# Query, score and choice pieces beside the expert gathers: one planned sequence becomes two streams with fixed places, and head 1's queries move ahead of the gathers

## The chip, the core and the metric

The kernel runs on one core of one Trainium2 chip. The metric is the device time of one execution in microseconds (us), as the median of the runs shown. One execution was taken by the hardware profiler; its times are the trace that everything below is read from.

## What is computed

Two transformer-like blocks on 256 tokens of width 1024, each with its own mixing branches. The change touches the last part of the second block alone, a retrieval of single-neuron experts. Cut to what matters:

```python
PEER_HEADS = 8; PEER_KEYS = 128; PEER_TOPK = 16
def _peer(h, w_q, sub_keys, u_emb, v_emb):
    q = (tok @ w_q).reshape(n_tok, PEER_HEADS, 2, PEER_HALF)
    s = jnp.einsum('nhpc,hpkc->nhpk', q, sub_keys)
    s_top, i_top = lax.top_k(s, PEER_TOPK)
    cand = s_top[:, :, 0, :, None] + s_top[:, :, 1, None, :]        # 16 x 16 per head
    best, pos = lax.top_k(cand, PEER_TOPK)
    expert = jnp.take_along_axis(cand_idx, pos, axis=-1)            # 16 experts per token and head
    gate = jax.nn.softmax(best, axis=-1)
    act = jax.nn.gelu(jnp.einsum('tkd,td->tk', u_emb[expert], tok)) * gate
    return jnp.einsum('tk,tkd->td', act, v_emb[expert])
x = x + _peer(_rmsnorm(x, norm2_g), ...)
return _rmsnorm(x, final_g)
```

Each token fetches 8 x 16 = 128 experts, and each expert is a row of 1024 numbers (u) and one of 1024 (v).

## The kernel before

Tokens lie in two blocks of 128 (b = 0, 1), one token per partition. The heads are worked in five groups (n): head 0, head 1, heads 2-3, 4-5, 6-7. An **item** is one gather of one expert per token of a block: 128 rows of 2048 numbers, 1 MiB, so 256 items in all. They come in the order group, block, head, expert: items 0-15 and 16-31 are head 0 (blocks 0 and 1), 32-63 head 1, 64-127 group 2, 128-191 group 3, 192-255 group 4.

`fetch` (L1470-1478) lets GpSimd (POOL) write and start the gather of an item into one of 8 slots of a ring (tag "uv", RING = 8). `use` (L1480-1492) is an item's work: VectorE (DVE) multiplies the u half with the token and sums (L1485, written into the slot itself), ScalarE (ACT) takes the gelu, the gate and a diagonal matrix `dg` (L1486, L1487, L1489), and TensorE (PE) adds dg x v to the block's sums `acc` with four matmul records (L1491). After that the slot is free for the gather eight items later.

Which expert rows a group needs is found by three kinds of pieces, which stand between the items:

- **queries** (`queries`, L1419-1441): four weight tiles of 128x1024 are split into a rounded part and a rest (L245 on ACT, then L246 on DVE; three buffers each), each is followed by 24 matmuls of 128x256 (L267-269), and the result `pq` is copied out by ACT (L1426). For head 1 the weights (wqa) are loaded here by SP's queue and there are two tiles; those of the other groups (wq) lie in SBUF.
- **scores** (`scores`, L1406-1416): the queries against the keys `sk` (L1412) into `psco`, copied by ACT into `s` (L1414).
- **choices** (`topk`, L1313-1369), once per group and block: per key half a best-16 piece (L1320-1324), per head a candidate piece (L1336 and again L1320-1324 on 256 wide rows), two one-hot pieces (L1341-1356, the second ends with `rows`, which the gathers read), and a softmax piece (L1364-1368: DVE `mx`, ACT exp with a table load, DVE reciprocal and `gate`).

`plan` (L1456-1461) chains all of them in one sequence: for each group its queries, scores, choices of block 0, choices of block 1. The main loop (L1506-1510) uses an item, takes one step of that sequence after items 0-7 and after every second later item (two of three between items 40 and 63), and fetches item i + 8; when its rows aren't there yet, `fetch` takes steps until they are. PE, DVE and ACT execute this part in the order in which it is written (`manual_schedule`). Every engine works through its own list in order, so an instruction that waits holds back all that is behind it on its engine.

Ahead of the loop, `first_queries` (L1284-1305) makes the queries and scores of head 0, and transposes the tokens into `acc` (L1304); then come the choices of (0, 0). `factors` and `tokens` (L1383-1397) make the normalized tokens `hn` with the norm weights `n2`, which lie in a weight buffer (tag "wf", four of them). This part, and all before, is put in order by the scheduler.

## Time and profile before

| | us |
|---|---|
| median of 3 runs (1533.45 to 1537.11) | 1534.99 |
| the profiled execution, whole | 1536.1 |
| its span in the trace | 1534.3 |
| first gather starts (POOL) | 852.1 |
| last product on DVE starts | 1522.9 |

The span is what the trace covers from its first to its last instruction, and 1.8 us of the whole lie around it. Busy shares over the whole span are PE 89%, DVE 68%, ACT 48%, POOL 20%, but they mix two very different parts: up to about 843 us PE multiplies almost without a pause, and from 852 us on the gathers run. Of the forty slices of the page, 38.4 us each, the transfer rate of the 24th to the 39th lies between 369 and 422 GB/s. A row of a timeline is: start, duration, engine, line, operation, output and inputs, number of instructions merged, and in brackets the idle time just before with what ended it. A row of a table by stretch holds for each engine the busy time and the number of instructions, then TensorE's granted clock, the share of the transfer engines, and GB/s.

### The profile page before, as it was taken

How to read it: one execution, taken by the hardware profiler on the slowest of the kernel's cores; microseconds unless marked ns; L12 is line 12 of the kernel's file. 1: busy time of each engine (PE TensorE's matmuls, PEld its weight loads, DVE VectorE, ACT ScalarE, POOL GpSimd, SP SyncE). 2: the span in 40 equal slices, each digit the busy share in tenths (PEclk: the TensorE clock that was granted, in tenths of full speed). 3: DMA queues.
4: the chain of work that ended last, by engine and by line, in shares of the span. 5: the costliest groups of instructions: out<-in, count | busy, mean ns of one | idle time of the engine just before them, and what ended most of it. 6: DMA issues, size and time to landing. Idle time of an engine off the chain costs nothing.

```text
span 1534.3 us, 21082 instructions
## 1 busy us (share of the span) xinstructions
PE 1359.4 (89%) x7496; PEld 975.3 (64%) x7496; DVE 1043.9 (68%) x2095; ACT 735.9 (48%) x1560; POOL 311.4 (20%) x277
## 2 busy tenths in 40 slices
PE   6999999989999999999999487877887888877786
PEld 3787799989999988989889142523533533322222
DVE  6775676867766778646387777588588588544543
ACT  7622454456555675534464435444443444433433
POOL 0000000000000000000010346344454455533341
PEclk9999999999999999999999799999999999999999
DMA  8655376745555453312155799999999999999996
GB/s 296 220 184 173 121 246 204 241 141 183 182 188 181 139 176 100 122 53 86 43 187 205 306 413 421 372 391 413 369 397 421 420 378 421 421 421 421 421 422 269
DMA packets 76712, 413.07 MB, mean 269 GB/s; under 512 B 8656, under 2 KB 9040, under 8 KB 43456
## 3 DMA queue, kind: packets, MB, share of 16 engines
q0 software_dynamic: 38880, 276.59, 44.2%
q1 hardware_dynamic: 37584, 134.88, 26.3%
q8 instruction: 59, 0.97, 0.2%
q14 instruction: 45, 0.37, 0.1%
q10 hardware_dynamic: 144, 0.26, 0.0%
HBM read 410.66 MB, written 1.05 MB: 268 GB/s over the span
## 4 chain that ended last, share of the span: by engine, by line
PE 55%; DVE 15%; DMA 11%; issue 9%; ACT 5%; POOL 5%; POOLq 0%; SPq 0%; DVEq 0%; ACTq 0%
PE psb L267 9%; PE psb L268 9%; PE psb L269 9%; DMA uv<-in_uv_dram,rows 9%; DVE uv L1485 6%; POOL uv L1478 5%; PE acc L1491 4%; PE psa L277 2%; PE psa L279 2%; PE psa L278 2%; DMA wf<-in_wmod_dram 2%; PE acc L267 1%; PE acc L268 1%; PE acc L269 1%; PE psr L1032 1%
## 5 line engine op out<-in xcount | busy, mean ns | idle before, releaser
L1491 PE MATMUL acc<-uv,dg 128*128 128x512 f32 x1024 | 495.3, 622 | 141.2 <-ACT dg L1489 140.7
L1491 PEld LDWEIGHTS acc<-uv,dg 128*128 128x128 f32 x1024 | 185.5, 194 | 438.2 <-ACT dg L1489 276.8
L1485 DVE CUSTOM_DVE_ANT_0 uv<-uv,hn 128x1024 f32<-128x1024 f32 x256 | 307.0, 1220 | 118.7 <-DMA uv<-in_uv_dram,rows 116.2
L1478 POOL DMA_INDIRECT uv<-in_uv_dram,rows x256 | 299.5, 1170 | 395.3 <-PE acc L1491 269.2
L246 DVE TENSOR_TENSOR wl<-wf,wh 128x1024 fp32r<-128x1024 f32 x213 | 258.2, 1216 | 134.4 <-ACT wh L245 131.6
L245 ACT CAST wh<-wf 128x1024 fp32r<-128x1024 f32 x213 | 221.9, 1044 | 240.4 <-PE psb L268 146.5
L267 PE MATMUL psb<-hxh,wh 128*128 128x256 f32 x960 | 280.8, 293 | 3.6 <-ACT hxh L370 3.4
L268 PE MATMUL psb<-hxl,wh 128*128 128x256 f32 x960 | 274.0, 286 | 0.0
L269 PE MATMUL psb<-hxh,wl 128*128 128x256 f32 x960 | 273.6, 286 | 0.2 <-DVE wl L246 0.2
L1486 ACT ACTIVATE act<-act 128x1 f32<-128x1 f32 x256 | 51.8, 202 | 325.1 <-DVE act L1485 325.1
L267 PEld LDWEIGHTS psb<-hxh,wh 128*128 128x128 f32 x960 | 184.9, 193 | 10.5 <-issue 5.2
L268 PEld LDWEIGHTS psb<-hxl,wh 128*128 128x128 f32 x960 | 184.9, 193 | 4.2 <-issue 3.3
L269 PEld LDWEIGHTS psb<-hxh,wl 128*128 128x128 f32 x960 | 184.6, 193 | 1.0 <-issue 0.3
L1489 ACT ACTIVATE dg<-io,act 128x128 f32<-128x128 f32 x256 | 102.8, 402 | 8.4
L1487 ACT ACTIVATE act<-act,gate 128x1 f32<-128x1 f32 x256 | 75.4, 294 | 8.3
L970 POOL MEMSET mt<- 128x2048 f32 x2 | 3.5, 1804 | 352.4 <-PE psb L268 352.4
L833 POOL DMA_DIRECT2D wq<-in_wq_dram x12 | 6.3, 529 | 262.4 <-PE pstm L982 142.8
L478 DVE SCALAR_TENSOR_TENSOR macc<-wf,cs,macc 128x512 f32<-128x512 f32 x56 | 41.9, 748 | 17.7 <-DMA wf<-in_wmod_dram 17.0
L267 PE MATMUL acc<-fh,wh 128*128 128x256 f32 x176 | 49.5, 281 | 0.0
L268 PE MATMUL acc<-fl,wh 128*128 128x256 f32 x176 | 49.5, 281 | 0.0
L269 PE MATMUL acc<-fh,wl 128*128 128x256 f32 x176 | 49.4, 281 | 0.0
L279 PE MATMUL psa<-wh,hxl 128*128 128x512 f32 x96 | 38.4, 400 | 0.0
(461 smaller groups left out, 2072.2 us busy)
## 6 DMA issues: line engine op xcount, KB each, us to landing
wf<-in_wmod_dram SPq DMA_DIRECT2D x48, 512.0 KB, 4.3
wf<-in_wup_dram SPq DMA_DIRECT2D x44, 512.0 KB, 3.6
wf<-in_win_dram SPq DMA_DIRECT2D x28, 512.0 KB, 4.5
wf<-in_wdn_dram SPq DMA_DIRECT2D x22, 512.0 KB, 3.7
wf<-in_wbg_dram SPq DMA_DIRECT2D x16, 512.0 KB, 4.4
wf<-in_wo_dram SPq DMA_DIRECT2D x16, 512.0 KB, 4.6
wf<-in_wml_dram SPq DMA_DIRECT2D x16, 512.0 KB, 3.5
wf<-in_wg_dram SPq DMA_DIRECT2D x16, 512.0 KB, 3.5
```

The source lines that it names most:

```text
L245: self.nc.scalar.copy(h, src)
L246: self.nc.vector.tensor_sub(l, src, h.bitcast(F32))
L267: nc.tensor.matmul(ps, p, xh[:, k0 + k, :], start=s, stop=False, skip_group_check=True)
L268: nc.tensor.matmul(ps, p, xl[:, k0 + k, :], start=False, stop=False, skip_group_check=True)
L269: nc.tensor.matmul(ps, q, xh[:, k0 + k, :], start=False, stop=e, skip_group_check=True)
L279: nc.tensor.matmul(ps, y, wh[:, k, :n], start=False, stop=e)
L1478: nc.gpsimd.indirect_dma_start(t, None, a["uv"], bass.IndirectOffsetOnAxis(ap=self.rows[b][:, h, k:k + 1], axis=0))
L1485: nc.vector.tensor_tensor_reduce(t[:, :D], t[:, :D], hn[:, b], 1.0, 0.0, ALU.mult, ALU.add, act)
L1486: nc.scalar.activation(act, act, AF.Gelu)
L1487: nc.scalar.activation(act, act, AF.Copy, scale=self.gate[b][:, h, k:k + 1])
L1489: nc.scalar.activation(dg, ident, AF.Copy, scale=act)
L1491: nc.tensor.matmul(acc[b][c], dg, t[:, D + c * 512:D + (c + 1) * 512], start=False, stop=h == PH - 1 and k == TOPK - 1, skip_group_check=True)
```

## The change

- Head 1's two weight tiles are loaded and split with head 0's, and `first_queries` makes head 1's queries and scores too, after the transposes into `acc`. Queries, keys and scores of both heads take three weight buffers; `n2` moves from a weight buffer into the ring's first slot. So 7 gathers start ahead of `tokens` and the 8th after it.
- The one sequence becomes two streams. Stream 0 holds the choices, each with a first item and a distance of 2 (1 for the first); stream 1 the queries and scores of groups 2, 3 and 4, from items 14, 70 and 134, one step every 4 items. The copy of `pq` stands one step (4 items) behind the last 24 matmuls, and the scores one step behind that copy.
- The softmax piece is cut in two: the reciprocal and `gate` stand one step behind `mx` and the exp.
- Behind the last item a Sqrt of one number per partition is added on ACT.

```diff
-        for _ in range(2):
-            self.ahead.append(self.weights(a["wqa"][0][:, 4 * len(self.ahead):4 * len(self.ahead) + 4], 256, 4))
+        for i in range(4):
+            self.ahead.append(self.weights(a["wqa"][i // 2][:, 4 * (i % 2):4 * (i % 2) + 4], 256, 4))
...
+        qs, sk, ss = (self.wp.tile([P, 1024], F32, tag="wf", name=n, bufs=4).rearrange("p (a t) -> p a t", t=P) for n in "qks")
+        nc.sync.dma_start(sk[:, :4], self.a["skt"][:, :4])
+        self.s0 = []
+        for h in range(2):
...
+            self.lin(self.a["wqa"][h], KT, 256, bs=[(self.scaled, cq)])
+            for b in range(NB):
...
+            if h:
+                break
+            for b in range(NB):
+                for k in range(KT):
+                    nc.tensor.matmul(self.acc[b][k // 4][:, k % 4 * P:(k % 4 + 1) * P], xt[:, k, b * P:(b + 1) * P], self.ident,
+                                     start=k % 4 == 0, stop=False, skip_group_check=True)
...
             nc.scalar.activation(bv[:, h], bv[:, h], AF.Exp, bias=mx[:, h:h + 1], scale=r, accum_out=sm[:, h:h + 1])
+        yield
         nc.vector.reciprocal(sm, sm)
...
-        n2 = self.wp.tile([P, 1024], F32, tag="wf", name="n2", bufs=4)
+        n2 = bp.tile([P, 2 * D], F32, tag="uv", name="n2", bufs=RING)[:, :D]
...
-            for k in range(2 if n == 1 else 4):
...
+            u = self.lin_units(None, KT, 512, bs=[(self.scaled, cq)])
+            for k in range(4):
+                self.ahead.append(self.weights(None, raw=next(wq)))
+                if k:
                     next(u)
                 yield
+            next(u)
+            yield
             for _ in u:
                 pass
             yield
             choices[n] = scores(q, sk, h0, nh)
             yield
...
-        def plan():
-            for n in range(len(heads)):
-                if n:
-                    yield from queries(n)
-                for b in range(NB):
-                    yield from run(n, b)
...
+        streams = [[], []]
+        for n, b, i, d in ((0, 1, 0, 1), (1, 0, 7, 2), (1, 1, 20, 2), (2, 0, 40, 2), (2, 1, 62, 2), (3, 0, 100, 2), (3, 1, 128, 2),
+                           (4, 0, 164, 2), (4, 1, 192, 2)):
+            streams[0].append([i, d, choose(n, b) if n < 2 else lambda n=n, b=b: choose(n, b)])
+        for n, i in ((2, 14), (3, 70), (4, 134)):
+            streams[1].append([i, 4, queries(n)])
...
-            for _ in range(RING):
+            for _ in range(RING - 1):
                 fetch()
+            next(start)
             tokens(0)
-            next(planned)
             tokens(1)
+            fetch()
+            for _ in start:
+                pass
             for i, w in enumerate(work):
                 use(w)
-                if i < 8 or (i % 3 if 40 <= i < 64 else i % 2):
-                    next(planned, None)
+                advance(0, i)
+                advance(1, i)
                 fetch()
+
+            nc.scalar.activation(self.warm, self.r[:, :1], AF.Sqrt)
```

Where the pieces stand is seen in each engine's list. **ACT, queries of group 2.** `pq` are the queries, `psb` the sums of the matmuls, `act` and `dg` an item's work, `s` the scores. Before:

```order
L1489 ACTIVATE dg_9585<-io_76,act_9581 128x128
L1486 ACTIVATE act_9591<-act_9591 128x1
L1487 ACTIVATE act_9591<-act_9591,gate0_8780 128x1
L1489 ACTIVATE dg_9595<-io_76,act_9591 128x128
L1426 COPY pq_9447<-psb_9477 128x512
L1426 COPY pq_9448<-psb_9478 128x512
L1486 ACTIVATE act_9627<-act_9627 128x1
L1487 ACTIVATE act_9627<-act_9627,gate0_8780 128x1
L1489 ACTIVATE dg_9631<-io_76,act_9627 128x128
L1414 COPY s_9640<-psco_9635 128x512
L1414 COPY s_9647<-psco_9642 128x512
```

After, the same copies of `pq`:

```order
L1483 ACTIVATE dg_9525<-io_76,act_9521 128x128
L1433 COPY pq_9158<-psb_9217 128x512
L1433 COPY pq_9159<-psb_9218 128x512
L1480 ACTIVATE act_9533<-act_9533 128x1
L1481 ACTIVATE act_9533<-act_9533,gate0_8851 128x1
L1483 ACTIVATE dg_9537<-io_76,act_9533 128x128
L1480 ACTIVATE act_9543<-act_9543 128x1
L1481 ACTIVATE act_9543<-act_9543,gate0_8851 128x1
L1483 ACTIVATE dg_9547<-io_76,act_9543 128x128
```

Before, one item stands between the two pairs of copies; after, four do (two are shown), and the copies of `pq` stand four items behind the last matmuls that they read.

**PE, ahead of the first item.** `acc<-io,xt` are the transposes, `psco` the scores, `psb` the queries. Before:

```order
L269 MATMUL psb<-hxh,wl 128x256
L1304 MATMUL acc<-io,xt 128x128 x4
L1300 MATMUL psco<-q 128x128 x4
L1304 MATMUL acc<-io,xt 128x128 x12
L1491 MATMUL acc<-uv,dg 128x512 x16
L267 MATMUL psb<-hxh,wh 128x256
```

After, first where the transposes end and then, 48 matmuls of L267-269 later, where the items begin:

```order
L1308 MATMUL acc<-io,xt 128x128 x4
L1301 MATMUL psco<-k,q 128x128 x4
L1308 MATMUL acc<-io,xt 128x128 x12
L267 MATMUL psb<-hxh,wh 128x256
L268 MATMUL psb<-hxl,wh 128x256
```

```order
L267 MATMUL psb<-hxh,wh 128x256
L268 MATMUL psb<-hxl,wh 128x256
L269 MATMUL psb<-hxh,wl 128x256
L1301 MATMUL psco<-k,q 128x128 x4
L1485 MATMUL acc<-uv,dg 128x512 x38
```

Head 1's 48 matmuls and its scores now stand behind the transposes and ahead of the first item.

**DVE, ahead of the choices of (0, 0).** `wl` is the rest of a weight tile, `hxl` the rest of the scaled tokens, `xt` the tokens. Before:

```order
L246 TENSOR_TENSOR wl<-wf,wh 128x1024 x3
L842 TENSOR_TENSOR xt<-psb,xt 128x512 x2
L379 SCALAR_TENSOR_TENSOR hxl<-xt,cv_5305,hxh 128x256 x4
L1320 MAX sv<-s 128x8 x2
L1321 MAX_INDEX si<-sv,s 128x8 x2
```

After:

```order
L246 TENSOR_TENSOR wl<-wf,wh 128x1024 x3
L842 TENSOR_TENSOR xt<-psb,xt 128x512 x2
L246 TENSOR_TENSOR wl<-wf,wh 128x1024
L379 SCALAR_TENSOR_TENSOR hxl<-xt,cv_5305,hxh 128x256 x4
L246 TENSOR_TENSOR wl<-wf,wh 128x1024
L1324 MAX sv<-s 128x8 x2
```

One of head 1's two rests stands ahead of `hxl`, the other behind it.

## Rows read from the trace of the kernel before

**Rows 1.** Table by stretch from the first full rate to the last gathers.

```profile
865.00:985.00 120.00, 100.17 (x303) 48.40 (x304) 84.22 (x198) 53.80 (x151) 54.63 (x42) 0.96 1.01 418
985.00:1000.00 15.00, 11.92 (x56) 7.67 (x55) 6.95 (x25) 6.79 (x21) 4.32 (x4) 1.00 0.71 260
1000.00:1090.00 90.00, 69.57 (x188) 30.70 (x187) 73.68 (x189) 42.10 (x122) 44.18 (x36) 1.00 1.01 412
1090.00:1125.00 35.00, 31.72 (x120) 17.89 (x119) 23.29 (x63) 14.32 (x46) 16.34 (x14) 1.00 0.89 335
1125.00:1225.00 100.00, 80.60 (x247) 38.53 (x245) 77.51 (x184) 44.17 (x129) 49.43 (x39) 1.00 1.01 422
1225.00:1250.00 25.00, 21.89 (x62) 10.60 (x63) 17.70 (x55) 12.12 (x40) 12.21 (x11) 1.00 0.93 351
1250.00:1510.00 260.00, 206.54 (x416) 74.11 (x414) 153.07 (x309) 104.39 (x332) 109.49 (x104) 0.97 1.01 421
```

**Rows 2.** Transfers issued from 820 us on: number, KB each, us to landing.

```profile
wf<-in_wqa_dram SPq DMA_DIRECT2D x4, 512.0 KB, 4.8
sk<-in_skt_dram SPq DMA_DIRECT2D x3, 256.0 KB, 7.5
```

**Rows 3.** Timeline around the first dip, DVE, ACT and POOL.

```profile
982.10 1.22 DVE L1485 CUSTOM_DVE_ANT_0 uv<-uv,hn 128x1024 f32<-128x1024 f32 x1
986.27 0.59 ACT L1426 COPY pq<-psb 128x512 f32<-128x512 f32 x1 [5.38 <-issue]
991.47 0.94 POOL L1478 DMA_INDIRECT uv<-in_uv_dram,rows  x1 [5.45 <-PE acc L1491]
992.13 0.58 ACT L1414 COPY s<-psco 128x512 f32<-128x512 f32 x1 [2.96 <-PE psco L1412]
992.74 0.29 DVE L1320 MAX8 sv<-s 128x8 f32<-128x128 f32 x1 [9.41 <-ACT s L1414]
```

**Rows 4.** Timeline of DVE: products with a split between them, then with a candidate piece.

```profile
1080.22 1.22 DVE L1485 CUSTOM_DVE_ANT_0 uv<-uv,hn 128x1024 f32<-128x1024 f32 x1
1083.41 1.22 DVE L246 TENSOR_TENSOR wl<-wq,wh 128x1024 fp32r<-128x1024 f32 x1 [1.97 <-ACT wh L245]
1084.56 1.22 DVE L1485 CUSTOM_DVE_ANT_0 uv<-uv,hn 128x1024 f32<-128x1024 f32 x1
...
1122.96 1.22 DVE L1485 CUSTOM_DVE_ANT_0 uv<-uv,hn 128x1024 f32<-128x1024 f32 x1
...
1126.95 1.21 DVE L1485 CUSTOM_DVE_ANT_0 uv<-uv,hn 128x1024 f32<-128x1024 f32 x1
```

**Rows 5.** Start of the gathers: two table rows (granted clock third from last), then timelines.

```profile
830.00:840.00 10.00, 10.00 (x86) 10.00 (x85) 5.32 (x8) 3.72 (x6) 0.00 (x0) 1.00 0.21 67
...
852.00:855.00 3.00, 0.00 (x0) 0.00 (x0) 2.38 (x6) 1.77 (x3) 2.26 (x3) 0.50 0.41 104
...
832.70 1.05 ACT L245 CAST wh<-wf 128x1024 fp32r<-128x1024 f32 x1 [1.74 <-PE psb L268]
...
836.27 1.66 DVE L379 SCALAR_TENSOR_TENSOR hxl<-xt,cv,hxh 128x256 fp32r<-128x256 f32 x4
...
843.03 2.84 PE L1304 MATMUL acc<-io,xt 128*128 128x128 f32 x24
...
852.13 1.00 POOL L1478 DMA_INDIRECT uv<-in_uv_dram,rows  x1 [38.48 <-issue]
...
855.00 0.33 SPq L257 DMA_DIRECT2D wf<-in_wqa_dram  x1
...
857.70 1.23 DVE L1485 CUSTOM_DVE_ANT_0 uv<-uv,hn 128x1024 f32<-128x1024 f32 x1 [2.73 <-DMA uv<-in_uv_dram,rows]
```

**Rows 6.** Timeline of ACT behind the last item.

```profile
1526.29 0.60 ACT L1519 ACTIVATE o<-acc 128x512 f32<-128x512 f32 x1 [1.22 <-PE acc L1491]
...
1527.92 1.28 ACT L1523 ACT_TABLE_LOAD   x1
...
1529.21 0.29 ACT L1523 ACTIVATE r<-r,eps 128x1 f32<-128x1 f32 x1
```

More of the change, by code (lines that the diff above doesn't have):

```diff
@@ L1287, in first_queries, with cq @@
         self.acc = [[self.ps("acc") for _ in range(2)] for _ in range(NB)]
[L1288 to L1305 removed]
+        qs, sk, ss = (self.wp.tile([P, 1024], F32, tag="wf", name=n, bufs=4).rearrange("p (a t) -> p a t", t=P) for n in "qks")
+        nc.sync.dma_start(sk[:, :4], self.a["skt"][:, :4])
+        self.s0 = []
+        for h in range(2):
+            q = qs[:, 4 * h:4 * h + 4].rearrange("p (i b) t -> p i (b t)", i=2)
+            def cq(ps, n0):
+                nc.scalar.copy(q, ps)
+            self.lin(self.a["wqa"][h], KT, 256, bs=[(self.scaled, cq)])
+            for b in range(NB):
+                s = ss[:, 4 * h + 2 * b:4 * h + 2 * b + 2]
+                ps = self.psd("psco").rearrange("p (a t) -> p a t", a=4)
+                for i in range(2):
+                    nc.tensor.matmul(ps[:, i], q[:, i, b * P:(b + 1) * P], sk[:, 2 * h + i], start=True, stop=True)
+                nc.scalar.copy(s, ps[:, :2])
+                self.s0.append(s)
+            if h:
[4 more added lines that the diff above has]
+                                     start=k % 4 == 0, stop=False, skip_group_check=True)
     def k2(self, shape, name, dt=F32):
@@ L1426, in cq @@
                 nc.scalar.copy(q[n0 // 2], ps)
-            for k in range(2 if n == 1 else 4):
-                if n == 1:
-                    w = self.weights(a["wqa"][1][:, 4 * k:4 * k + 4], 256, 4)
-                else:
-                    w = self.weights(None, raw=next(wq))
-                self.ahead.append(w)
-                if k == 0:
-                    u = self.lin_units(None, KT, 256 * nh, bs=[(self.scaled, cq)])
-                else:
+            u = self.lin_units(None, KT, 512, bs=[(self.scaled, cq)])
+            for k in range(4):
+                self.ahead.append(self.weights(None, raw=next(wq)))
+                if k:
                     next(u)
                 yield
+            next(u)
+            yield
             for _ in u:
@@ L1443, in queries, with choose @@
             yield
-        choices = {}
-        todo = []
+        choices = {n: [self.topk(self.s0[2 * n + b], b, n, 1) for b in range(NB)] for n in range(2)}
         done = set()
-        def run(n, b):
+        def choose(n, b):
             for p in choices[n][b]:
@@ L1454, in run @@
                 yield
-        def plan():
-            for n in range(len(heads)):
-                if n:
-                    yield from queries(n)
-                for b in range(NB):
-                    yield from run(n, b)
-        planned = plan()
         work = [(n, b, h, k) for n, (h0, nh) in enumerate(heads) for b in range(NB) for h in range(h0, h0 + nh) for k in range(TOPK)]
@@ L1475, in fetch @@
             while (n, b) not in done:
-                next(planned)
+                advance(0)
             tiles[w] = t = bp.tile([P, 2 * D], F32, tag="uv", name="uv", bufs=RING)
@@ L1492, in use, with advance @@
                                  stop=h == PH - 1 and k == TOPK - 1, skip_group_check=True)
+        streams = [[], []]
[4 more added lines that the diff above has]
+            streams[1].append([i, 4, queries(n)])
+        def advance(j, i=None):
+            st = streams[j]
+            if st and (i is None or i >= st[0][0]):
+                x = st[0]
+                if callable(x[2]):
+                    x[2] = x[2]()
+                x[0] += x[1]
+                if next(x[2], 0) == 0:
+                    st.pop(0)
+                    advance(j, i)
         self.first = None
-        choices[0] = [self.topk(self.s0[b], b, 0, 1) for b in range(NB)]
+        start = choose(0, 0)
         factors()
```

19 lines of the change are left out of this document (1 added, 18 removed).

## The prediction

> **What bounds the kernel now.** I first read the transfer rate of the forty slices on the page, then a table by stretch of the part that the change touches, then the timelines of its dips, its start and its end. Between 1250 and 1510 us the transfers run at 421 GB/s with all 16 engines full, while PE, DVE and ACT have time to spare [rows 1]. An item is 128 x 2048 x 4 bytes = 1.049 MB, so the plateau gives one item per 1.049 / 0.421 = 2.49 us, and 256 of them need 637 us. Nothing that the engines do makes this stage shorter than that; what the change can win is where the rate falls below the plateau, plus bytes that aren't gathers, plus what stands ahead of and behind the stage.
>
> The rate falls at three places [rows 1]. Counted as (421 - rate) / 421 x length: 985 to 1000 us loses 161/421 x 15 = 5.7 us, 1090 to 1125 us 86/421 x 35 = 7.1, 1225 to 1250 us 70/421 x 25 = 4.2: 17.0 in all. The stretches beside them lose little: 865 to 985 us 0.9, 1000 to 1090 us 1.9, and 1125 to 1225 us nothing. Together 19.8 us.
>
> The timeline shows what the first dip is [rows 3]. ACT reaches the copy of `pq` and stands 5.38 us, since PE still has to do the last 24 query matmuls, which are behind items. Behind that copy on ACT are the items' gelu and `dg`, and PE's `acc` matmuls wait for those. One item later the score copy waits another 2.96 us for PE. DVE has run ahead through landed tiles, the last at 982.10, and stands 9.41 us in front of the first best-16 piece, which wants those scores. So slots come free late: POOL waits 5.45 us for PE before it starts the gather of 991.47, where one every 2.49 us is wanted. The eight slots run dry and the rate falls. The other two dips fall on the queries and scores of groups 3 and 4, which are written the same way.
>
> **The change part by part.** The sum is made against the profiled execution: 1536.1 us, of which 1534.3 are the span. Its differences are then put on the median of 1534.99, 1.1 below it.
>
> *The three dips.* In the new order the last 24 matmuls of a group, the copy of `pq` and the scores are each 4 items apart, that is 4 x 2.49 = 10 us at the plateau; the copy's wait was 5.38 us and the scores' 2.96 [rows 3], so both are over before ACT arrives. The first best-16 piece stands two items behind the scores for group 2 (items 38 and 40) and six for groups 3 and 4 (94 and 100, 158 and 164). Two items are 5 us, against 2.96 for PE's scores plus 0.58 for a copy. The waits that emptied the ring go: 19.8 us.
>
> *What is late next.* Query steps now run beside choices, so DVE gets both. From the product starts [rows 4]: an item alone takes 1.14 us (the rest of two neighbours' spacing), an item with a split 1084.56 - 1080.22 = 4.34, so a split adds 3.20, of which 1.97 is the wait for ACT's rounding; an item with a candidate piece takes 1126.95 - 1122.96 = 3.99, so that piece adds 2.85. Where a split stands behind a piece, ACT rounds during the piece, and the split adds 1.22. I price each one-hot piece at the candidate's 2.85 as a bound. The worst place is items 70 to 79: a pair of items has 2 x 2.49 = 4.98 us; items 70-71 need 2.28 + 2.85 + 1.22 = 6.35, 72-73 need 5.13, 74-75 6.35, 76-77 5.13, 78-79 2.28 + 3.20 = 5.48. DVE falls behind by 1.37 + 0.15 + 1.37 + 0.15 + 0.50 = 3.5 us and then catches up, since a pair without a piece needs 2.28. Items 134 to 143 are alike. What the ring forgives is read from the first dip: DVE stood 9.41 us and the transfers lost 5.7 there, or 7.6 with the stretch behind it, so 1.8 to 3.7 us are forgiven [rows 1, 3]. A loss between nothing and 2 x (3.5 - 1.8) = 3.4 us is left; the stretch of 1125 to 1225 us, which held splits at every second item at 422 GB/s, is nearest, so I take 1.0. PE is not near its limit: 24 query matmuls at 86 in 10 us [rows 5] are 2.8 us, now once in 10 us.
>
> *Could rows come too late?* A choice takes eight steps at every second item, so group 2's rows for block 0 are written behind item 54 and first fetched behind item 56; the others have 6 to 12 items to spare. DVE writes them ahead of the products whose slot that gather needs, so the slot still comes last. Nothing.
>
> *Bytes.* One of head 1's two weight loads (0.52 MB) starts at 855.00, when gathers already run [rows 5]; it now comes earlier, and so does one key load of 0.26 MB [rows 2]. 0.79 MB at 421 GB/s are 1.9 us less; between 0 (were they moved in a gap that is there anyway) and 1.9 I take 1.9, since the first gathers are in flight at 855.
>
> *Ahead of the first gather.* Added are two loads, two splits, 48 matmuls, a copy of `q`, four score matmuls and two copies. The 48 matmuls, 48 x 0.116 = 5.6 us [rows 5], stand behind the transposes, which end at 843.03 + 2.84 = 845.87 [rows 5]; PE is free from there until the first product, which DVE begins at 857.70. They and the scores end near 853, and ACT's exp, now behind their copies, near 855: hidden while the first gather is on its way, which costs 5.6 us from its start at 852.13. If that cover were gone they would cost some 8 us. The first new split is not hidden: ACT's cast of 1.05 us needs the buffer that the last `w_out` matmuls free, about 2.8 us after the one before it was let go at 832.70, so it begins near 835.5 and delays the scaled tokens by 0.9; on DVE its rest of 1.22 us stands ahead of `hxl` and moves it from 836.27 to about 837.8. PE needs those only for its second 24 query matmuls, from about 838.2; I estimate 0.3 us, between 0 and the 1.5 by which `hxl` moves. On SP's queue the keys for group 2 wait for the second split, and `n2` is queued behind them: it starts near 841 and is wanted by `tokens` at 852. The ring's first slot is held by `n2`, so the eighth gather waits for `tokens`, about 855; POOL comes to it at about 861. Nothing.
>
> *The end.* The Sqrt's table load of 1.28 us stands on the path at 1527.92 [rows 6]. It now runs in the 1.22 us that ACT waits until 1526.29; load and Sqrt take 1.28 + 0.29 = 1.57 and so push the squares back by about 0.4, so 0.9 are won, between 0 and 1.28. Between that load's start and the next instruction's at 1529.21 lie 1.29 us [rows 6]. The Trainium skill (ScalarE: Activation LUTs, What ACT_TABLE_LOAD costs) gives 1283 ns for such a load and another 1380 ns for a drain, some 2.7 us for each switch; the trace agrees on the load and shows no drain behind it. With the page's drain the gain would be an estimated 1.4 us more and the sum -22.7 (1512.3); I keep to the row.
>
> *The softmax piece.* DVE no longer waits for the exp. At the plateau such waits are covered by the ring: nothing.
>
> **Sum.** -19.8 + 1.0 - 1.9 + 0.3 - 0.9 = -21.3 us. The profiled execution would take 1514.8, the median 1513.7. With each term at its good end it is 19.8 + 1.9 + 1.3 = 23.0 less, 1512.0; with each at its bad end 19.8 - 3.4 - 1.5 = 14.9 less, 1520.1.
>
> **The rivals.** *The overlap empties the ring.* If queries beside choices drain the slots twice (items 70-82 and 134-146), each as deep as the mildest dip of before, 4.2 us, the gain on the dips is 19.8 - 8.4 = 11.4 and the time 1534.99 - 11.4 - 1.9 - 0.9 + 0.3 = 1521.1. For it: DVE needs up to 6.35 us per 4.98 there, and a late PE adds to it. Against: the dips came from a wait of 9.41 us, and no wait of that kind is left.
>
> *The dips stay.* POOL starts each gather itself, in 0.94 us alone [rows 3]. The Trainium skill (SBUF — State Buffer, the "DVE blocks DMA" trap) says that some DVE operations lock GpSimd out of a shared port while it writes descriptors; by that rule work of DVE beside the gathers, of which the change leaves as much as there was, makes the dips. In the trace DVE stood idle in the first dip and POOL waited for PE's `acc`, not for DVE [rows 3], which speaks against POOL and DVE as the cause. As a mechanism of this kernel: if the dips are POOL's and stay, only bytes, end and start count, 1534.99 - 1.9 - 0.9 + 0.3 = 1532.5.
>
> *Slower: the front comes onto the path.* Should the products wait for all of head 1's front work, that is two splits of 1.05 + 1.22 (4.5 us), 48 matmuls (5.6, or 11.2 at the granted clock of 0.50 that PE has at 852 us, after its pause) and, on SP's queue, a key load of 7.5 and the norm weights behind it at about 4.8 (a weight load's landing), the first product comes 22.4 to 28.0 us later. From 21.6 us on it eats up the gain (21.3 and the 0.3 already counted); at the near end the time is 1535.8, at the far end 1534.99 - 21.6 + 28.0 = 1541.4. Against it: PE has 11.8 us free between 845.87 and 857.70, and SP's two loads run while DVE still chooses.
>
> **How the numbers follow.** Forecast 0.81, overlap 0.12, dips stay 0.04, slower 0.03. A measurement of this kernel can tell about 0.2%, 3.1 us, from no change. Faster by more: 0.81 + 0.12 and half of the third case, 0.95; the other half within, 0.02; slower 0.03. The range goes from 1511.0 (1 us below the good end, for what 855 to 865 us may give) to 1522.0, which takes in the overlap; some 0.1 to 0.15 is left outside.
>
> **What would show it.** Right: no stretch of 15 us between 870 and 1490 us below 400 GB/s; copies of `pq` and best-16 pieces that wait under 1 us; first gather at 852 to 854; no table load behind the last item's `acc`. Wrong: dips at items 70-82 or 134-146 with DVE busy (overlap), dips with POOL busy (descriptors), or a first product later than 859 (front).

## The result, and the profile after

The changed kernel takes 1519.64 us in the median (1517.43 to 1521.7, 4 runs), the kernel before beside it 1536.05 (1533.45 to 1538.03, 4 runs): a ratio of 0.9894, 95% interval 0.9872 to 0.9916, or 16.4 us less. The forecast was 21.3 us less and 1513.7; the time lies in the range, 6 us above the forecast. The profiled execution is the run of 1517.43, its span 1515.7.

First the table by stretch, with the stretches of [rows 1] and two more at the end. Columns: the stretch, its length, busy time and instructions of PE, PE's weight loads, DVE, ACT and POOL, then granted clock, share of the 16 transfer engines, GB/s.

```profile
865.00:985.00 120.00, 101.12 (x300) 47.87 (x300) 91.33 (x235) 57.21 (x164) 58.07 (x47) 0.99 1.01 421
985.00:1000.00 15.00, 9.90 (x23) 3.99 (x23) 14.09 (x35) 5.42 (x18) 6.61 (x6) 1.00 1.01 419
1000.00:1090.00 90.00, 75.62 (x234) 36.91 (x233) 65.02 (x148) 44.01 (x127) 37.97 (x35) 0.98 1.01 416
1090.00:1125.00 35.00, 30.56 (x79) 12.94 (x77) 20.62 (x49) 13.80 (x45) 17.01 (x16) 1.00 1.01 418
1125.00:1225.00 100.00, 77.69 (x183) 30.58 (x184) 77.67 (x190) 40.76 (x125) 41.07 (x39) 1.00 1.01 421
1225.00:1250.00 25.00, 23.66 (x107) 14.93 (x107) 15.32 (x27) 14.23 (x40) 11.61 (x9) 1.00 1.01 401
1250.00:1490.00 240.00, 186.33 (x402) 68.81 (x400) 149.52 (x329) 98.86 (x310) 101.43 (x97) 1.00 1.01 422
1490.00:1500.00 10.00, 7.94 (x16) 2.71 (x16) 4.93 (x8) 3.63 (x13) 0.78 (x1) 1.00 0.77 321
1500.00:1515.00 15.00, 7.93 (x16) 2.71 (x16) 5.47 (x10) 6.48 (x17) 0.00 (x0) 0.98 0.11 43
```

The three dips of [rows 1] are gone: 260, 335 and 351 GB/s are now 419, 418 and 401. Two shallow ones are left, which the long stretches hide:

```profile
1071.00:1086.00 15.00, 15.00 (x61) 8.92 (x60) 9.51 (x15) 7.23 (x22) 8.38 (x8) 1.00 0.99 390
1235.00:1250.00 15.00, 15.00 (x71) 9.77 (x70) 9.81 (x16) 6.34 (x21) 7.61 (x6) 1.00 1.00 388
```

Counted as in the prediction, the stretches of [rows 1] now lose 2.6 us rather than 19.8; with the bytes the stage should have given some 19 of the 20.7 us forecast for it (dips, overlap and bytes). It gave 15.7: from the first item's product to the last item's it took 665.15 us (857.70 to 1522.85) and takes 649.45. The last product before, and then the first and the last after:

```profile
1522.85 1.22 DVE L1485 CUSTOM_DVE_ANT_0 uv<-uv,hn 128x1024 f32<-128x1024 f32 x1 [1.24 <-DMA uv<-in_uv_dram,rows]
```

```profile
855.71 1.23 DVE L1479 CUSTOM_DVE_ANT_0 uv<-uv,hn 128x1024 f32<-128x1024 f32 x1 [1.93 <-DMA uv<-in_uv_dram,rows]
...
1505.16 1.23 DVE L1479 CUSTOM_DVE_ANT_0 uv<-uv,hn 128x1024 f32<-128x1024 f32 x1 [1.24 <-DMA uv<-in_uv_dram,rows]
```

To find the other 5 us of the forecast I read something that the prediction didn't: the **landings**. Where a product waited for its own gather (`<-DMA uv` in DVE's timeline), its start tells when that gather had landed. From each such start I take off the first product's start and 2.488 us, the plain spacing, for each item. What is left is how far the landings have fallen behind. It hardly ever goes back in either kernel, and in the kernel after it grows in steps:

| loss in us | before | after | difference | predicted |
|---|---|---|---|---|
| items 0 to 35 | 8.7 | 5.4 | -3.3 | -2.8 (bytes 1.9, first stretch 0.9) |
| items 35 to 159 | 18.8 | 4.8 | -14.0 | -17.9 (dips and the stretch beside them 18.9, overlap +1.0) |
| items 159 to 255 | 3.2 | 4.8 | +1.6 | 0 |
| whole stage | 30.7 | 15.0 | -15.7 | -20.7 |

The 15.0 us of after: 2.3 at item 1; 1.0 at 9; 2.2 at 31 (938 us); nine steps of 0.91 to 0.97 at items 57, 70, 93, 116, 146, 168, 192, 212 and 246; and 0.6 and 0.5 at 229 and 230, where the first block's outputs are written. One such step, in DVE's timeline:

```profile
1339.53 1.23 DVE L1479 CUSTOM_DVE_ANT_0 uv<-uv,hn 128x1024 f32<-128x1024 f32 x1 [1.26 <-DMA uv<-in_uv_dram,rows]
...
1342.01 1.23 DVE L1479 CUSTOM_DVE_ANT_0 uv<-uv,hn 128x1024 f32<-128x1024 f32 x1 [1.25 <-DMA uv<-in_uv_dram,rows]
...
1345.46 1.23 DVE L1479 CUSTOM_DVE_ANT_0 uv<-uv,hn 128x1024 f32<-128x1024 f32 x1 [2.21 <-DMA uv<-in_uv_dram,rows]
```

Products come 2.48 apart, then once 3.45. No stretch of the table shows it: 1250 to 1490 us, with four of the steps and the two at the outputs, stands at 422 GB/s. An item's gather is spread over the 16 transfer engines and is there when the last of them is done, while the rate is their mean: the ones ahead go on to the next gather. They give it back at the end, where the rate falls to 321 and then 43 GB/s while landings still come every 2.49 us to 1505. There one engine of the 16 is alone at work (a share of 0.06), and it sets the landings:

```profile
1500.00:1504.00 4.00, 3.50 (x8) 1.35 (x8) 2.47 (x4) 0.94 (x4) 0.00 (x0) 1.00 0.06 27
```

The transfers of 1336 to 1346 us (queue: packets, MB, share of 16 engines) show what else was under way:

```profile
q0 software_dynamic: 578, 4.20, 101.3%
q14 instruction: 1, 0.01, 0.2%
```

One packet of instructions, 8 KB. I found such a packet ahead of most steps, but not a step behind every packet. The step at item 93 has none near ahead of it; in both repeats of this kernel that step stands at item 97, behind one. That was a correlation; the experiments were made to test it.

### The profile page after: what moved, and what is told of

Read it like the earlier page. It is cut to its first block, busy times and chain, and to the rows that moved or that the text cites. A ratio compares the mean times of both kernels' runs of the same rounds, so it can differ in the third digit from the quotient of the medians.

```text
span 1515.7 us, 21089 instructions
## 1 busy us (share of the span) xinstructions
PE 1350.3 (89%) x7496; PEld 969.3 (64%) x7496; DVE 1047.1 (69%) x2095; ACT 737.7 (49%) x1561; POOL 295.2 (19%) x277
## 4 chain that ended last, share of the span: by engine, by line
PE 50%; DMA 19%; DVE 12%; issue 11%; POOL 5%; ACT 4%; POOLq 0%; DVEq 0%; SPq 0%; ACTq 0%
DMA uv<-in_uv_dram,rows 18%; PE psb L267 8%; PE psb L268 8%; PE psb L269 8%; POOL uv L1472 5%; DVE uv L1479 4%; PE acc L1485 2%; PE psa L277 2%; PE psa L279 2%; PE psa L278 2%; PE acc L267 1%; PE acc L269 1%; PE acc L268 1%; ACT wh L245 1%; PE psr L1032 1%
## 5 line engine op out<-in xcount | busy, mean ns | idle before, releaser
L1485 PE MATMUL acc<-uv,dg 128*128 128x512 f32 x1024 | 488.5, 614 | 131.3 <-ACT dg L1483 128.8
L1485 PEld LDWEIGHTS acc<-uv,dg 128*128 128x128 f32 x1024 | 182.1, 191 | 426.7 <-ACT dg L1483 268.2
L1479 DVE CUSTOM_DVE_ANT_0 uv<-uv,hn 128x1024 f32<-128x1024 f32 x256 | 310.2, 1222 | 172.8 <-DMA uv<-in_uv_dram,rows 165.9
L1472 POOL DMA_INDIRECT uv<-in_uv_dram,rows x256 | 283.3, 1107 | 396.0 <-PE acc L1485 264.9
L267 PE MATMUL psb<-hxh,wh 128*128 128x256 f32 x960 | 279.3, 291 | 4.2 <-ACT hxh L370 3.4
L267 PEld LDWEIGHTS psb<-hxh,wh 128*128 128x128 f32 x960 | 184.2, 192 | 10.7 <-issue 4.7
L267 PE MATMUL acc<-fh,wh 128*128 128x256 f32 x176 | 49.5, 281 | 0.0
L277 PE MATMUL psa<-wh,hxh 128*128 128x512 f32 x96 | 38.4, 400 | 0.0
```

The source lines that it names most:

```text
L267: nc.tensor.matmul(ps, p, xh[:, k0 + k, :], start=s, stop=False, skip_group_check=True)
L277: nc.tensor.matmul(ps, x, wh[:, k, :n], start=s, stop=False)
L1472: nc.gpsimd.indirect_dma_start(t, None, a["uv"], bass.IndirectOffsetOnAxis(ap=self.rows[b][:, h, k:k + 1], axis=0))
L1479: nc.vector.tensor_tensor_reduce(t[:, :D], t[:, :D], hn[:, b], 1.0, 0.0, ALU.mult, ALU.add, act)
L1485: nc.tensor.matmul(acc[b][c], dg, t[:, D + c * 512:D + (c + 1) * 512], start=False, stop=h == PH - 1 and k == TOPK - 1, skip_group_check=True)
```

## The experiments

All times are medians, and a loss is read from the one trace of its kernel. The kernel before, on the same chip, took 1537.12 us beside the first four kernels below; 1535.8 beside the tiny instructions on ACT, the copies in one step, the front alone and the early factors; and 1539.06 beside the rest. Kernels that did not run side by side are compared by their ratios. The theories at the start: **A**, the landings are held back by what else the transfer engines carry (instruction packets, small transfers); **B**, by DVE's pieces, the prediction's own overlap.

**The changed kernel again.** No edit.

> The changed kernel again, unaltered, as the measure for the three kernels beside it: 1517 to 1522 us. Both theories say the same of it: no stretch of 15 us between 870 and 1490 below 400 GB/s, and yet landings that fall back against the plain pace of 2.488 us an item by 9 to 10 us between items 35 and 255, in steps of about 0.95 us.

1521.05 us, ratio 0.9901 (0.9869 to 0.9933). Loss 14.8 us, with steps of the same size at the same items to within four (56, 70, 97, 116, 146, 168, 192, 212, 229, 230, 246). The steps belong to the program, not to one execution. So do the two shallow dips, 391 and 388 GB/s over 15 us: that no stretch would fall below 400 was wrong.

**Items alone.** The diff is cut: in `fetch` and `use`, which are not shown, every item takes group 0's rows and gates.

```diff
-        for n, b, i, d in ((0, 1, 0, 1), (1, 0, 7, 2), (1, 1, 20, 2), (2, 0, 40, 2), (2, 1, 62, 2), (3, 0, 100, 2), (3, 1, 128, 2),
-                           (4, 0, 164, 2), (4, 1, 192, 2)):
+        for n, b, i, d in ((0, 1, 0, 1),):
...
-        for n, i in ((2, 14), (3, 70), (4, 134)):
+        for n, i in ():
```

> The changed kernel with the queries, scores and choices of groups 1 to 4 left out; every item takes group 0's rows and gates, so it gathers the same 256 times but repeated rows. Theory A (the stage's landings are held back by what else the DMA engines carry, instruction packets and small transfers, about 0.95 us each): shorter instruction lists, so 2 to 6 us less than the changed kernel, and the 0.95-us steps that stay stand at the packets that stay. Theory B (VectorE's choice pieces and weight rests hold the gathers): no piece is left, so about 5 us less and no steps at all between items 35 and 228. Where neither holds and 2.49 us an item with its steps is simply the price of a gather, within 1 us of the changed kernel.

1513.93 us, ratio 0.9844 (0.9812 to 0.9876); loss 8.9 us. Even with nothing but items five steps of 0.79 to 0.97 stay, at items 70, 102, 134, 166 and 198: every 32 items. B's "no steps at all" has fallen. So has "simply the price of a gather", since the time is 7.1 below the changed kernel's, a little more than A's 2 to 6.

**Eight tiny instructions with each item, on DVE.** The same kernel, and in `use`, behind the product:

```diff
+            for j in range(8):
+                nc.vector.memset(tiny[:, j:j + 1], 0.0)
```

> The kernel with the choices left out (group 0's rows and gates for all items), and eight VectorE memsets of 128x1 with each item: 2048 more instructions and no transfer of their own. VectorE is busy some 1.2 us of an item's 2.49 there, so the memsets fit beside it. Theory A: more instruction packets on the DMA engines, so more steps of about 0.95 us: 4 to 15 us over the kernel without the memsets. Theory B: no long VectorE piece, so within 1 us of it.

1526.77 us, ratio 0.9931 (0.9907 to 0.9956): 12.8 over items alone, and the loss 22.1 rather than 8.9. The page's line on the instruction queue q14 (packets, MB, share), of items alone:

```profile
q14 instruction: 42, 0.34, 0.1%
```

The same line of this kernel:

```profile
q14 instruction: 57, 0.47, 0.1%
```

DVE's timeline at one of this kernel's steps:

```profile
1099.70 1.23 DVE L1481 CUSTOM_DVE_ANT_0 uv<-uv,hn 128x1024 f32<-128x1024 f32 x1 [1.13 <-DMA uv<-in_uv_dram,rows]
1103.16 1.23 DVE L1481 CUSTOM_DVE_ANT_0 uv<-uv,hn 128x1024 f32<-128x1024 f32 x1 [2.10 <-DMA uv<-in_uv_dram,rows]
```

2048 more instructions are 15 more packets; the steps go from 9 to 24 in number, 15 more, nearly all of them of 0.94 to 1.01 us. They come every 11 to 12 items, 1.6 to 2.6 us behind packets that come every 30 us. DVE itself still waits 188.3 us for gathers between 1000 and 1400 us, so it isn't late. Nor do the memsets hold up POOL: its issue of a gather takes 954 ns in the mean, and 961 without them. A is confirmed in size and place. At the end one transfer engine again works alone, for longer than in the kernel after:

```profile
1507.00:1513.00 6.00, 4.93 (x11) 1.74 (x11) 3.77 (x21) 1.80 (x6) 0.00 (x0) 1.00 0.06 27
```

**No rest.** Of the twelve weight splits beside the gathers, the DVE half is left out and the rounded half used twice.

```diff
-        self.split(wf, wh, wl)
+        if raw is None:
+            self.split(wf, wh, wl)
+        else:
+            nc.scalar.copy(wh, wf)
+            wl = wh
```

> The changed kernel without the VectorE half of the twelve weight splits beside the gathers; the rounded half is used in its place, so the queries of heads 2 to 7 are less exact and some rows differ. Twelve pieces of 128x1024 less on VectorE, the pieces that the prediction priced at 0 to 3.4 us. Theory A: within 1 us of the changed kernel. Theory B: 1 to 5 us less.

1519.64 us, ratio 0.9879 (0.9848 to 0.9909), loss 15.3 us, the same number of steps. The time is 1.4 us below the changed kernel beside it. By the number alone that would be B's, but both spread wider (1517.71 to 1521.36 here, 1519.17 to 1525.53 there), and the stage is no shorter: 649.7 us from first to last product, 649.2 there. Twelve pieces of 1.2 us less on DVE buy nothing that can be measured, and B has fallen. They do remove the first shallow dip:

```profile
1071.00:1086.00 15.00, 15.00 (x61) 8.88 (x60) 7.53 (x13) 6.33 (x19) 8.03 (x8) 1.00 1.01 422
```

So DVE's overlap makes that dip, and the dip costs the landings nothing.

**Five tiny instructions with each item, on ACT.** In the kernel with items alone three series of q14 packets come at periods of about 80, 80 and 160 us, and only one has steps behind it. With the memsets it is one of the two at 80 that came closer together. So the question was whether packets of any engine's list cost something, or those of DVE's alone.

```diff
+            for j in range(5):
+                nc.scalar.copy(tiny[:, j:j + 1], self.eps)
```

> The kernel with the choices left out (group 0's rows and gates for all items), and five ScalarE copies of 128x1 with each item: 1280 more instructions on ScalarE, none on VectorE. ScalarE is busy 0.9 us of an item's 2.49 there, so they fit beside it. Theory A1 (every instruction packet beside the gathers costs a step): some ten packets more, 8 to 10 us over the kernel without the copies. Theory A2 (only packets of VectorE's list cost one; in the kernel without the copies the landings step at one of three series of packets alone, and with the memsets it was that series which came closer together): more packets, within 1.5 us of the kernel without the copies, and no step added.

1515.86 us, ratio 0.9871 (0.9832 to 0.991), loss 12.1 rather than 8.9. By the landings both A1 and A2 are wrong. Ten packets more (52 on q14), and from item 60 on the steps are of another size, 0.53 to 0.69 us, one every 14 or 15 items, while none of 0.95 is left. DVE's timeline at one of them:

```profile
1291.81 1.22 DVE L1481 CUSTOM_DVE_ANT_0 uv<-uv,hn 128x1024 f32<-128x1024 f32 x1 [1.26 <-DMA uv<-in_uv_dram,rows]
1294.97 1.22 DVE L1481 CUSTOM_DVE_ANT_0 uv<-uv,hn 128x1024 f32<-128x1024 f32 x1 [1.93 <-DMA uv<-in_uv_dram,rows]
```

What fits all of these is **A3**: the packets of one engine's list set one transfer engine behind, by some 0.95 us each for DVE's and 0.66 for ACT's, and only the transfer engine that is furthest behind sets the landings; losses of different lists aren't added. Here ACT's 17 packets in the stage, 17 x 0.66 = 11.2, have passed DVE's 7, 7 x 0.95 = 6.7, which are hidden now. That the lists go to different transfer engines is inferred: the records don't name the engine.

The trace's records of single transfers, each with its start and length, bear A3 out. A gather's transfer of 8 KB takes 0.31 us in the median. In the kernel after, eleven of them beside the items take 0.96 or 0.97 us, and each begins where a q14 packet of 0.33 us ends, within 0.02 us. Behind packets of another series the next transfer takes 0.68 to 0.70; of these there are 7 with items alone and 17 with the copies on ACT. So a packet, with what the transfer behind it loses, costs its engine some 0.97 us in the one series and 0.68 in the other, near the two sizes of the steps. At the end of the kernel with the copies on ACT two engines are at work from 1497 to 1498 us (a share of 0.12) and one from 1499 to 1502 (0.06): more than one list has set an engine behind.

**The copies in one step with the matmuls.** This and the next undo parts of the change.

```diff
-            next(u)
-            yield
             for _ in u:
                 pass
```

> The changed kernel with one of its edits undone: the last 24 matmuls of a query sequence and the two copies of its result stand in one step again, as in the kernel before, so a copy can wait on ScalarE for the matmuls while gates of items stand behind it. The spacing of the two streams stays. Theory of the prediction (the copies' wait empties the ring): the three dips are back, 5 to 15 us over the changed kernel, with stretches of 15 us below 400 GB/s near 1000, 1140 and 1300. Rival (the spacing of the steps alone ended the dips, the copies' place is worth nothing): within 1.5 us of the changed kernel and no stretch below 400 GB/s.

1519.15 us, ratio 0.9901 (0.9868 to 0.9934), loss 14.9, the same steps. ACT's timeline at group 3 shows that the waits are back:

```profile
1087.83 0.59 ACT L1433 COPY pq<-psb 128x512 f32<-128x512 f32 x1 [6.86 <-PE psb L269]
...
1098.83 0.59 ACT L1420 COPY s<-psco 128x512 f32<-128x512 f32 x1 [5.55 <-PE psco L1418]
```

DVE's longest waits between 865 and 1500 us (waited for: us, times, longest us); none is for scores:

```profile
DVE uv L1477 <- DMA uv<-in_uv_dram,rows: 154.2, 128, 2.2
DVE wl L246 <- ACT wh L245: 16.9, 8, 4.6
```

The copies' waits, 2.9 to 6.9 us in the three groups, cost nothing by themselves while query steps stand four items apart. Behind two of them the rate falls to 379 and 383 GB/s over 15 us (from 1095 and from 1257 us), so the rival's "no stretch below 400" was wrong too, but the landings lose no more. The prediction had put such a wait at the head of the chain that made the dip. That theory has fallen.

**The front alone.** Head 1 stays ahead of the gathers; beside them there is a single sequence again.

```diff
+        def plan():
+            for n in range(len(heads)):
+                if n > 1:
+                    yield from queries(n)
+                for b in range(NB):
+                    if n or b:
+                        yield from choose(n, b)
...
-                advance(0, i)
-                advance(1, i)
+                if i < 8 or (i % 3 if 40 <= i < 64 else i % 2):
+                    advance(0)
```

> The changed kernel with the part beside the gathers put back to a single sequence, pulled at every second or third item as in the kernel before (the last matmuls and the copies in one step again); head 1's queries and scores stay ahead of the gathers, and so does the last table load. Theory of the prediction (the streams end the dips, the move of head 1 is worth 2 us or so): the dips after 985, near 1100 and near 1230 are back, 1531 to 1535 us. Rival (the dips came from head 1's queries beside the gathers, whose going sets the others free): 1519 to 1523 us, as the changed kernel.

1527.94 us, ratio 0.9953 (0.9933 to 0.9974), loss 24.3: the dips are back as steps of 7.7, 3.8 and 3.1 at items 76, 108 and 160. So the parts that stay (head 1's move, bytes, table load, the cut softmax piece) are worth 7.9 us, three to seven more than expected, and the streams the other 8 to 9. In the landings 3.8 us of it lie ahead of item 35, and most of the rest in shallower dips. DVE's waits for scores between 865 and 1500 us in the kernel before:

```profile
DVE sv L1320 <- ACT s L1414: 35.4, 4, 11.1
```

In this one:

```profile
DVE sv L1324 <- ACT s L1420: 26.3, 3, 11.1
```

In the kernel after and in the one with the copies at once the same view lists none. That alone doesn't make this wait the cause: the next run has dips without it.

**Queries at every second item.** The copies in one step as above, and

```diff
-            streams[1].append([i, 4, queries(n)])
+            streams[1].append([i, 2, queries(n)])
```

> The changed kernel with the last matmuls and the copies in one step, and a query step at every second item rather than every fourth; choices as they are. Theory (one wait of 6 to 7 us on ScalarE is taken up by the items in flight, two that end within 8 us of one another empty the ring; with a step at every fourth item they ended 11 to 12 us apart, in the single sequence 7.6): the waits for copies and scores end some 6 to 8 us apart and the landings lose 4 to 8 us more than the changed kernel's 15, so 1523 to 1528 us. Rival (what empties the ring is a query's waits together with choice pieces behind them): within 1.5 us of the changed kernel.

1531.75 us, ratio 0.996 (0.9938 to 0.9982): 11.5 over the changed kernel beside it, and a loss of 27.9. No choice waits for scores here, yet the ring empties, and not for the reason that I gave. At group 3 the waits of copies and scores end 10.7 us apart (1077.45 and 1088.12), as far as in the kernel with the copies at once (11.0), which has no deep dip. The difference is on PE. Its timeline, from one query step to the next but one:

```profile
1062.82 0.68 PE L267 MATMUL psb<-hxh,wh 128*128 128x256 f32 x1
...
1066.09 3.60 PE L1483 MATMUL acc<-uv,dg 128*128 128x512 f32 x8
1069.12 0.68 PE L267 MATMUL psb<-hxh,wh 128*128 128x256 f32 x1
...
1072.39 3.59 PE L1483 MATMUL acc<-uv,dg 128*128 128x512 f32 x8
1075.42 0.68 PE L267 MATMUL psb<-hxh,wh 128*128 128x256 f32 x1
```

The table's row of the dip, columns as above:

```profile
1080.00:1090.00 10.00, 7.18 (x24) 3.97 (x24) 3.70 (x6) 4.00 (x11) 1.88 (x2) 0.83 0.71 267
```

The timeline of a gather issued in the dip, and of its product:

```profile
1092.78 0.94 POOL L1470 DMA_INDIRECT uv<-in_uv_dram,rows  x1 [4.37 <-PE acc L1483]
...
1098.45 1.23 DVE L1477 CUSTOM_DVE_ANT_0 uv<-uv,hn 128x1024 f32<-128x1024 f32 x1 [3.56 <-DMA uv<-in_uv_dram,rows]
```

PE goes from one to the other without a wait there: a query step and two items come every 6.30 us (1062.82, 1069.12, 1075.42), and the gathers want two items in 4.98. So PE falls behind by 1.3 us a step. With a step at every fourth item such a round is about as long as the four items' 9.95 us: 1063.44, 1074.56 and 1084.29 in the kernel after, with 1.1 us idle in the first round and none in the second. The kernel before has the rhythm of 6.30 us, and its timeline shows it just ahead of its second dip:

```profile
1079.01 0.68 PE L267 MATMUL psb<-hxh,wh 128*128 128x256 f32 x1
...
1082.28 3.59 PE L1491 MATMUL acc<-uv,dg 128*128 128x512 f32 x8
1085.31 0.68 PE L267 MATMUL psb<-hxh,wh 128*128 128x256 f32 x1
...
1091.61 0.68 PE L267 MATMUL psb<-hxh,wh 128*128 128x256 f32 x1
...
1097.90 0.68 PE L267 MATMUL psb<-hxh,wh 128*128 128x256 f32 x1
```

PE has no idle time from 1079.01 to 1097.90, nor in the same rounds ahead of the third dip (1202.51 to 1221.40). Ahead of the first, two rounds with one item each take 4.58 us against 2.49, and one with two items 6.30. In the kernel with the denser queries the gather of 1092.78 was in use 5.7 us later, as long as a gather takes with nothing ahead of it (5.4 for the first, 850.27 to 855.71 in the kernel after): the ring was empty. In the kernel after the shortest such time beside the items is 9.3 us, with the copies at once 8.4.

**The last norm's factors early.**

```diff
         nc.sync.dma_start(n2, a["n2r"].to_broadcast([P, D]))
+        fg = bp.tile([P, D], F32, name="fg")
+        nc.sync.dma_start(fg, a["fg"].to_broadcast([P, D]))
...
-        fg = self.wp.tile([P, 1024], F32, tag="wf", name="fg", bufs=4)
-        nc.sync.dma_start(fg, a["fg"].to_broadcast([P, D]))
```

> The changed kernel with the 0.5 MB of the last norm's factors loaded ahead of the gathers, behind the other norm's, into a tile of its own, rather than at 919 us beside them. Theory A (every byte and packet that the DMA engines carry beside the gathers is paid in full by the landings): the step of 2.2 us that the landings take at 938 us falls to about 1, the loss between items 0 and 255 from 15 to about 13.8, and the time by about 1.2 us. Theory B (the load fills gaps of the gathers): the loss stays at 15. Rival to both: the load delays the first gather by up to 1.2 us, and the time stays.

1518.27 us, ratio 0.9883 (0.9847 to 0.9919). In the landings it is as A has it: the step of 2.2 at 938 us is 0.93 now, the loss 13.3 rather than 14.4 to 15.0. In the time the intervals overlap, so 1.4 us isn't shown there.

**A column for each activation, with the early load.** Each product then waits for two semaphores rather than three.

```diff
+        acts = bp.tile([P, len(work)], F32, name="acts")
...
-            act = kp.tile([P, 1], F32, tag="a", name="act", bufs=6)
+            act = acts[:, len(used):len(used) + 1]
```

> The changed kernel with the last norm's factors loaded ahead of the gathers, and with a column of its own for each item's activation, so that the item's product waits for two semaphores rather than three. Theory A3 (each list's instruction packets put one DMA engine behind, VectorE's by 0.95 us each and ScalarE's by 0.66, and the engine furthest behind sets the landings): if the third wait takes a slot in VectorE's list, 256 slots less are two packets less, the landings lose about 11.4 us between items 0 and 255 rather than 13.3, and the time is 1.5 to 2.5 us below that of the kernel with the early load alone, 3 to 4 below the changed kernel. Rival (a wait takes no slot, or the packets have no part in it): 13.3 us lost, the same time as with the early load alone.

1518.93 us, ratio 0.989 (0.9864 to 0.9917), and the unaltered changed kernel beside it 1520.21, 0.9886 (0.9862 to 0.991): no difference that these runs can tell. The loss is 12.4 us, 0.8 under the early load alone, with one packet less on q14 (44 for 45) and one step less, where I expected two. That is the direction of my guess that a third wait takes a slot in the list, at half of its size and in one trace of each; a version faster than the changed kernel isn't shown.

The changed kernel beside it:

> The changed kernel again, unaltered, beside the kernel with the early load and a column for each activation: 1518 to 1522 us.

As expected (1517.29 to 1521.85, loss 14.4).

**Without the last square root.**

```diff
-            nc.scalar.activation(self.warm, self.r[:, :1], AF.Sqrt)
```

> The changed kernel without the square root of one value that stands behind the last item on ScalarE. The table load is back behind the last output's squares, between them and the square root of the norm: from the last product's start to the end of the span 11.4 us as in the kernel before, rather than 10.5, and 0.9 us more in the time. Rival (the load is paid either way): 10.5 us and no difference.

From the last product's start to the end of the span 11.6 us (1507.99 to 1519.6), against 10.5 in the changed kernel; the time is 1521.81 against 1520.21, the direction right, the size within what the two spread. ACT's timeline, with the load on the path again as in [rows 6]:

```profile
1513.06 1.28 ACT L1542 ACT_TABLE_LOAD   x1
1514.35 0.29 ACT L1542 ACTIVATE r<-r,eps 128x1 f32<-128x1 f32 x1
```

The kernel after, ahead of the squares:

```profile
1507.42 1.28 ACT L1531 ACT_TABLE_LOAD   x1
1508.71 0.20 ACT L1531 ACTIVATE warm<-r 128x1 f32<-128x1 f32 x1
1508.82 0.58 ACT L1539 ACTIVATE o<-acc 128x512 f32<-128x512 f32 x1
...
1510.45 0.30 ACT L1543 ACTIVATE r<-r,eps 128x1 f32<-128x1 f32 x1 [0.23 <-DVE r L1542]
```

## Why the prediction was right, and where it was 5 us off

**What bounds the kernel: right in kind, too low.** The stage is bound by the gathers. But its floor isn't 2.49 us an item: with items alone 8.9 us are lost beside it, of which 1.1 at the output writes and most of the rest in steps behind instruction packets. The plateau of 421 GB/s can't show that.

**The dips: size right, cause half right.** By the rate they and the stretch beside them cost 18.9 us behind item 35, and by the landings 18.8. But not all of this was there to win. The kernel before fetches instructions too, and its landings show no separate step between items 35 and 159 but two jumps of 14.5 and 4.4. A ring that runs dry takes such a loss in, since the engine that is behind catches up: at the end of the kernel before the last engine is alone for little over 1 us, in the kernel after for 5. In the kernel after the stretch loses five steps, 4.8 us. On the cause, [rows 3] showed two waits in a chain, ACT's for `pq` and DVE's of 9.41 us for the scores. The prediction began the chain at ACT's. The waits for `pq`, put back, cost nothing. DVE's wait for scores goes with the dips of the single sequence (35.4 us before, 26.3 with the front alone), but it isn't needed: with query steps at every second item the ring ran dry without it, at a loss 13.0 us above that of the copies at once, from which that kernel differs in this alone. What the kernels with deep dips share is PE's rhythm of 6.30 us for a query step and two items, without idle time and against 4.98. PE stands in the prediction only as "not near its limit ... now once in 10 us", which is so of the kernel after; that PE was at its limit ahead of each dip of before, it did not see. So the streams end the dips because they halve the density of the query steps, more than by the places of the copies. Whether the wait for scores deepens the dips stays open.

**What is late next: the step that failed.** This term was +1.0, for DVE's overlap, with 0 to 3.4 as bounds. The overlap did come, and more of it: DVE's product of item 79 starts 6.1 us behind the pace of the landings and that of item 147 3.9, where 3.5 was forecast, and the rate falls to 390 and 388 GB/s, by the prediction's count 2.3 us. It cost the landings nothing: no step at items 71 to 87 or 147 to 159, and none saved without the rests. What the rate lost there can only have been the lead of engines that were ahead. What was late next was the transfer engine furthest behind: 4.8 us between items 35 and 159, and 1.6 more than before behind them, where the kernel has four steps of 0.95 rather than three of 0.6 to 1.0; the choices now run later there, which may be why. So the term measured 6.4, 5.4 too small, and that is the stage's miss of 5.0 us, but for the 0.5 won at the start. The bounds missed it because they came from rates, and a rate is a mean over 16 engines.

**Bytes: right, as far as can be told.** Up to item 35 the loss fell by 3.3, against 2.8 for the bytes and the first stretch together.

**The front: right.** The first gather starts at 850.27 rather than 852.13, but the work ahead of it, which the change doesn't touch, was about 2.0 us earlier in this execution; that leaves +0.1, predicted +0.3. `hxl` starts at 835.79, 836.27 in [rows 5], so against the work ahead of it 1.5 us later, as predicted. The sign "852 to 854" missed by this shift.

**The end: right.** From the last product's start to the end 11.5 us before and 10.5 after: -1.0, predicted -0.9. The load takes 1.28 us and the next instruction starts 0.01 behind it. The Trainium skill (ScalarE: Activation LUTs, What ACT_TABLE_LOAD costs) adds a drain to each switch; neither this trace nor the one without the square root shows one.

**Sums.** Stage -15.7, end -1.0, front +0.1: -16.6, and the medians differ by 16.4. That they agree so closely is partly chance: the first product alone stands at 855.71, 857.64 and 860.07 us in three traces of the changed kernel.

**The rivals.** The overlap's rival gave 1521.1, closer to the time than the forecast, but by luck: the two dips that it named are there, shallow and just behind its items, and the landings lose nothing at them. Dips that stay, and a front on the path, didn't occur: the first product is at 855.71.

**The signs.** No stretch of 15 us below 400 GB/s: missed, 390 and 388. It would have proved little either way, since these two stretches cost nothing and the 5 us were lost at 421. Copies of `pq` that wait under 1 us: right. No table load behind the last `acc` on the path: right.

## What to carry to other kernels

A mean transfer rate at its plateau doesn't say that nothing is lost: where each item needs all transfer engines, take the landing times against the plain spacing, and look for steps. Price what removing a dip brings against the small losses that the dip now hides, and not against the plateau. Of a chain of waits, the first isn't the cause because it is first: put each link back alone. And lay the rhythm of each engine, busy without a gap, beside the pace of the transfers (6.30 us against 4.98): an engine that is idle on average can be the limit for a few rounds.

## What was not expected of the hardware

- Instruction packets of 8 KB travel on the engines that move the data, and in this gather stage each of VectorE's costs the landings 0.95 us (15 more packets, 15 more steps, 12.8 us), though a packet itself takes 0.2% of 16 engines in 10 us, that is 0.32 us. The rest is in the gather's transfer right behind the packet, which takes 0.97 us rather than 0.31; why isn't known.
- For ScalarE's packets the step is 0.66 us, and it shows only once its list is the one that is furthest behind.
- A ring of eight 1 MB gathers took waits of 6 to 7 us on ScalarE without loss (the copies at once); it ran dry where TensorE was 1.3 us late on every two items, round after round.
